# Attention by pairs of key blocks: two blocks' transposes back to back, their products with V together at the step's end

## The chip, the cores and the metric

The kernel runs on one core of a Trainium2 chip. The metric is the device time of one execution in microseconds (us), given as the median of several runs; less is better.

## The reference

One layer of a two-branch attention block on 1024 positions of width 1024, all in float32. An input projection feeds branch A (latent attention, 8 heads, mask by chunks of 64) and branch B (attention with a forget gate, 8 heads, causal). What the change touches is the inner part of both:

```
for i in range(seq // Q_BLOCK):            # blocks of 128 queries
    lo, hi = i * Q_BLOCK, (i + 1) * Q_BLOCK
    s = (scores of q[lo:hi] with k[:hi]) * scale   # + bias in branch B
    s = jnp.where(mask, s, -jnp.inf)
    p = jax.nn.softmax(s, axis=-1)
    outs.append(jnp.einsum('bhqk,bkhd->bqhd', p, v[:, :hi]))
```

The outputs are multiplied by SiLU gates, projected, merged with sigmoid gates, projected once more and added to the input.

## The kernel before, in words

Every large product is made of float32r matmuls: operands are split into a high and a low part, and three (sometimes two) products are summed in PSUM. The program first normalizes the input and makes the latents (0 to about 290 us of the profile), then runs the attention of all 16 heads with the remaining projections between (about 290 to 812 us), then the rest of the projections and the output.

**Order of the work.** All engines follow the order in which the program is written. `attention` (L1254) walks over 16 heads and, for each, over 12 *turns*, one for each block of keys `j`: four for the first half of the queries (`g` = 0, blocks 0 to 3) and eight for the second (`g` = 1, blocks 0 to 7). A counter of modelled TensorE time (`pe_time`) is advanced by each matmul; a turn is due every `STEP` = 2490 of it, and `fill_to` (L142) puts matmuls of the projections (tiles `f`) between until the time is reached. So TensorE always has projection work behind the attention work, in a fixed order.

**A turn** (`turn`, L1195) transposes the block of P (the softmax's result, rows of queries) with one transpose for each of up to four query blocks, into a bank of PSUM `pt` (tag `t`, two buffers). ScalarE copies it to the high part of `pp` (L1207), VectorE makes the low part (L1208). `product` multiplies both with V into the bank `o`, one or two turns later, from a queue in `attention`. For the blocks on the diagonal (the last four of each half) only 4, 3, 2 and 1 query blocks remain, so tiles are 512, 384, 256 and 128 columns wide.

**The scores of later rows** are made between the turns by `scores` (L1158), in an order that the table `ahead` gives: rows of 128 queries, 0 to 3 of a head in the PSUM tile `n` (one buffer), 4 to 7 in the tile `s` (1024 columns, **one buffer** during attention). After the matmuls VectorE takes the maximum (L1181), ScalarE the exponential from PSUM into SBUF with the sum (L1187, two records on the engine: ACTIVATE and ACTIVATION_READ_ACCUMULATOR), VectorE the reciprocal (L1190), GpSimd scales (L1191). The exponential is issued by the first `next` on the generator that `scores` returns, the scaling by the second. In the loop before, the first `next` comes in the turn after the scores, right after that turn's transposes and copy, and new scores are begun after it:

```
pr = self.turn(n, g, j)
last, finish = finish, None
if last:
    next(last)            # exponential of the scores begun a turn ago
...
if k in ahead and n + ahead[k][0] < N:
    finish = self.scores(n + ahead[k][0], ahead[k][1])
```

The rows 4, 5, 6 of the next head and 7 of this one, which share the one `s` buffer, are begun in turns 7, 9, 11 and 1: two turns apart.

**Preparation of the next heads' q and k** (`prep_a`, `prep_b`; groups of four transposes into a `t` bank, tiles `qt`, `kt`) is called at turns given by the table `parts`.

Of the kernel before, what the change touches and what calls it, by code (L numbers as in the profile page):

```python
# [74 lines left out]
class Net:  # L75
# [966 lines left out]

    def prep_a(self, n):

        nc, U = self.nc, self.U
# [144 lines left out]
            yield  # L1192
        return finish()

    def turn(self, n, g, j):  # L1195
# [2 lines left out]
        i0 = max(j - 4 * g, 0)
        c0 = i0 * P
        pt = self.bank("t", f"pt{n}_{g}{j}")  # L1200
        for i in range(i0, 4):
            self.transpose(pt[:, i * P:(i + 1) * P], self.p[n, 4 * g + i][:, j * P:(j + 1) * P])
        if j >= 4 * g:
            (self.U if g else self.Hs).put(self.p.pop((n, j)))
        pp = self.U.get([P, 2, 512], F32R, f"pp{n}_{g}{j}")
        ph, pl = pp[:, 0], pp[:, 1]
        nc.scalar.copy(ph[:, c0:], pt[:, c0:])  # L1207
        nc.vector.tensor_tensor(out=pl[:, c0:], in0=pt[:, c0:], in1=ph[:, c0:].bitcast(F32), op=ALU.subtract)  # L1208

        def product():  # L1210
            v = self.v[n]
            if j == 0:
                self.o = self.bank("o", f"o{n}_{g}")
            o = self.o
            self.U.put(pp)
            if j < 4 * g + 3:
                self.mm(o[:, c0:], v[:, j], ph[:, c0:], j == 0, False)
                self.mm(o[0:64, c0:], v[:, j, 0:64], pl[:, c0:], False, False)
                return
            self.mm(o[0:64, c0:], v[:, j, 0:64], pl[:, c0:], False, False)  # L1220
            self.mm(o[:, c0:], v[:, j], ph[:, c0:], False, True)
# [32 lines left out]
    def attention(self):  # L1254
        nc, N = self.nc, len(self.seq)
        preps = {n: self.prep_a(n) if n < 8 else self.prep_b(n) for n in range(0, N, 2)}
        parts = {}
# [4 lines left out]
        next(preps[0])
        self.fill_to(self.pe_time + 10000)
        self.load_v(0)
        for i in range(5):
# [4 lines left out]
            if i == 4:  # L1270
                self.gate_sum((4, 5))
                self.gate_load((6, 7))
        for c, i in enumerate((0, 4, 1, 5, 2, 3, 6)):
# [16 lines left out]
            self.fill_to(self.pe_time + 1500)  # L1290
        due = self.pe_time
        ahead = {1: (0, 7), 2: (1, 0), 4: (1, 1), 6: (1, 2), 8: (1, 3), 7: (1, 4), 9: (1, 5), 11: (1, 6)}
        for n in range(N):
            for k in range(12):
                g, j = (0, k) if k < 4 else (1, k - 4)
                due += self.STEP
                pr = self.turn(n, g, j)
                last, finish = finish, None
                if last:
                    next(last)  # L1300
                if (n, k) in parts:
                    next(preps[parts[n, k]])
                if k in ahead and n + ahead[k][0] < N:
                    finish = self.scores(n + ahead[k][0], ahead[k][1])
                if last:
                    next(last)
                if k == 2 and 0 < n < N - 1:
# [1 line left out]
                for at, call, a in self.extra:
                    if at == (n, k):  # L1310
                        call(*a)
                self.fill_to(due - 600)
                if k not in (1, 5):
                    while queue:
                        queue.pop(0)()
                self.fill_to(due)
                queue.append(pr)
# [38 lines left out]
    def build(self):  # L1356
# [35 lines left out]
        self.extra += [((3, 0), self.gate_row, ())]  # L1392
# [125 lines left out]
```

## Time and profile before

| | |
|---|---|
| Runs | 966.36, 964.3, 965.95 us; median 965.95 |
| Profiled execution | 961.75 us; span from first to last instruction 959.9 us |
| TensorE matmul (PE) | 947.9 us busy, 99% of the span, granted clock 0.999 |
| VectorE (DVE), ScalarE (ACT), GpSimd (POOL) | 66%, 50%, 22% of the span |
| Chain that ended last | PE 92%, DMA 3%, DVE 2%, ACT 2% |

How to read it: matmuls are pipelined, so a record of one lasts longer (0.40 us for 512 columns) than the distance from one start to the next (0.23 us); prices of TensorE are therefore read from starts. The name of a group is out<-in without buffer numbers. "Idle before" is time in which the engine did nothing before an instruction, with what ended it.

### The profile page before, as it was taken

How to read it: one execution, taken by the hardware profiler on the slowest of the kernel's cores; microseconds unless marked ns; L12 is line 12 of the kernel's file. 1: busy time of each engine (PE TensorE's matmuls, PEld its weight loads, DVE VectorE, ACT ScalarE, POOL GpSimd, SP SyncE). 2: the span in 40 equal slices, each digit the busy share in tenths (PEclk: the TensorE clock that was granted, in tenths of full speed). 3: DMA queues.
4: the chain of work that ended last, by engine and by line, in shares of the span. 5: the costliest groups of instructions: out<-in, count | busy, mean ns of one | idle time of the engine just before them, and what ended most of it. 6: DMA issues, size and time to landing. Idle time of an engine off the chain costs nothing.

```text
span 959.9 us, 14942 instructions
## 1 busy us (share of the span) xinstructions
PE 947.9 (99%) x5390; PEld 820.6 (85%) x5390; DVE 633.2 (66%) x1379; ACT 477.3 (50%) x959; POOL 208.1 (22%) x260
## 2 busy tenths in 40 slices
PE   7999999999999999999999999999999999999998
PEld 7999999998878888888888888888888888888887
DVE  3977877778366667657667676667676766495222
ACT  7776624543245556556555566465565654143000
POOL 0022142200012222221233333232333220046000
PEclk9999999999999999999999999999999999999999
DMA  9831132951973225235332232222421554644321
GB/s 340 334 98 45 51 114 62 323 216 40 343 232 110 88 67 132 71 95 133 99 91 68 66 101 89 80 88 89 120 70 46 186 186 154 238 147 138 103 88 66
DMA packets 79961, 124.96 MB, mean 130 GB/s; under 512 B 5928, under 2 KB 47536, under 8 KB 79888
## 3 DMA queue, kind: packets, MB, share of 16 engines
q1 hardware_dynamic: 79888, 124.01, 39.4%
q8 instruction: 42, 0.69, 0.3%
q14 instruction: 31, 0.25, 0.1%
HBM read 88.33 MB, written 35.66 MB: 129 GB/s over the span
## 4 chain that ended last, share of the span: by engine, by line
PE 92%; DMA 3%; DVE 2%; ACT 2%; issue 1%; SPq 1%; POOL 0%; ACTq 0%; DVEq 0%; POOLq 0%
PE f L127 36%; PE out L127 9%; PE s L127 9%; PE b L127 8%; PE o L127 7%; PE pt L136 6%; PE q L127 3%; PE ckv L127 2%; PE kv L127 2%; PE cq_s L127 2%; PE bv L127 1%; PE cq_t L127 1%; DMA x_u<-in_x 1%; PE pada L127 1%; DMA va_d<-vhl_u 1%
## 5 line engine op out<-in xcount | busy, mean ns | idle before, releaser
L1207 ACT CAST pp_u<-pt 128x512 fp32r<-128x512 f32 x192 | 91.9, 479 | 171.1 <-PE pt L136 155.0
L1208 DVE TENSOR_TENSOR pp_u<-pt,pp_u 128x512 fp32r<-128x512 f32 x192 | 106.7, 556 | 84.8 <-ACT pp_u L1207 81.9
L127 PE MATMUL f<-hT_lo,hi_f_u 128*128 128x512 f32 x384 | 153.6, 400 | 0.0
L127 PE MATMUL f<-hT_hi,lo_f_u 128*128 128x512 f32 x384 | 153.4, 399 | 0.0
L127 PE MATMUL f<-hT_hi,hi_f_u 128*128 128x512 f32 x384 | 153.1, 399 | 0.0
L127 PE MATMUL s<-k_u,q_u 96*128 96x512 f32 (+6 forms) x480 | 116.8, 362 | 0.9 <-DMA k_u<-kr_d 0.9
L1181 DVE TENSOR_REDUCE nm<-s 128x1 f32<-128x128 f32 (+7 forms) x128 | 97.0, 758 | 4.4
L1191 POOL TENSOR_SCALAR p_u<-p_u,rs 128x640 f32<-128x640 f32 (+1 forms) x64 | 64.3, 1004 | 164.1 <-DVE rs L1190 119.0
L1191 POOL TENSOR_SCALAR p_h<-p_h,rs 128x128 f32<-128x128 f32 (+1 forms) x64 | 41.7, 652 | 247.3 <-DVE rs L1190 208.2
L127 PE MATMUL o<-pp_u,v_u 128*128 128x512 f32 (+7 forms) x384 | 94.2, 340 | 0.0
L127 PEld LDWEIGHTS s<-k_u,q_u 96*128 96x128 f32 (+2 forms) x480 | 77.0, 190 | 7.3 <-issue 0.9
L127 PEld LDWEIGHTS f<-hT_hi,hi_f_u 128*128 128x128 f32 x384 | 72.4, 189 | 12.1
L127 PEld LDWEIGHTS f<-hT_hi,lo_f_u 128*128 128x128 f32 x384 | 72.4, 189 | 11.2
L127 PEld LDWEIGHTS f<-hT_lo,hi_f_u 128*128 128x128 f32 x384 | 72.5, 189 | 11.1
L127 PEld LDWEIGHTS o<-pp_u,v_u 128*128 128x128 f32 (+1 forms) x384 | 61.8, 161 | 19.5
L127 PE MATMUL b<-hi_b_u,hT_hi 128*128 128x256 f32 x256 | 73.1, 285 | 0.0
L127 PE MATMUL b<-hi_b_u,hT_lo 128*128 128x256 f32 x256 | 72.4, 283 | 0.0
L127 PE MATMUL b<-lo_b_u,hT_hi 128*128 128x256 f32 x256 | 72.4, 283 | 0.0
L136 PEld LDWEIGHTS pt<-ident,p_u 128*128 128x128 f32 x416 | 52.7, 140 | 16.7
L136 PE MATMUL pt<-ident,p_u 128*128 128x128 f32 x416 | 66.2, 272 | 0.0
L1187 ACT ACTIVATE p_u<-s,nm 128x640 f32<-128x640 f32 (+1 forms) x64 | 61.5, 961 | 4.3 <-DVE nm L1181 3.2
L127 PE MATMUL out<-lo_wo_u,hT_hi 128*128 128x512 f32 (+1 forms) x136 | 51.2, 377 | 0.0
(318 smaller groups left out, 2073.1 us busy)
## 6 DMA issues: line engine op xcount, KB each, us to landing
raw_f_u<-in_w_t SPq DMA_DIRECT2D x24, 512.0 KB
wada_u<-in_w_ada SPq DMA_DIRECT2D x16, 512.0 KB
mg_d<-th_h SPq DMA_DIRECT2D x32, 256.0 KB
mg_h<-mg_d SPq DMA_DIRECT2D x32, 256.0 KB
x_u<-in_x SPq DMA_DIRECT2D x8, 512.0 KB
raw_b_u<-in_w_b SPq DMA_DIRECT2D x8, 512.0 KB
raw_wg_u<-in_w_gate SPq DMA_DIRECT2D x8, 512.0 KB
va_d<-vhl_u SPq DMA_DIRECT2D x8, 512.0 KB
```

The source lines that it names most:

```text
L127: self.nc.tensor.matmul(out, lhsT=l, rhs=r, start=start, stop=stop)
L136: self.nc.tensor.transpose(out=out, in_=in_, identity=self.ident)
L1181: nc.vector.tensor_reduce(out=nm, in_=sv, axis=AX.X, op=ALU.max, negate=True)
L1187: nc.scalar.activation(p[:, 0:w], sv, AF.Exp, bias=nm, accum_out=sm)
L1191: nc.gpsimd.tensor_scalar(out=p[:, 0:w], in0=p[:, 0:w], scalar1=rs, scalar2=0.0, op0=ALU.mult, op1=ALU.add)
L1207: nc.scalar.copy(ph[:, c0:], pt[:, c0:])
L1208: nc.vector.tensor_tensor(out=pl[:, c0:], in0=pt[:, c0:], in1=ph[:, c0:].bitcast(F32), op=ALU.subtract)
```

## The change

A head now has six *steps* instead of twelve turns; a step takes two blocks of keys. Steps 0 and 1 are blocks (0,1) and (2,3) of the first half; steps 2 to 5 are blocks (0,1), (2,3), (4,5), (6,7) of the second. At the start of a step the transposes of both blocks stand back to back, then the two copies and the two subtractions. For the last pair of a half the two narrow blocks (256 and 128 columns) are put side by side into one bank, so that one copy and one subtraction of 384 columns serve both. The products of both blocks are made at the end of the same step (800 of modelled time before it is due), right before the next step's transposes. The order of high and low product is low, high except for block 0. What follows a half (`ends`) is issued at the start of the next step, after the transposes.

The scores that are begun at a step's start get their exponential inside the step (at 2900 before it is due). In steps 3 and 4 a second row is begun at that point (`ahead2`: rows 4 and 5 of the next head, tile `s`); its exponential is issued at the start of the next step, after the transposes and copies. Row 6 (also tile `s`) is begun at the start of step 5. The table `parts` is written anew for the steps; the call of `gate_row` moves by one place.

```diff
+    def turn(self, n, g, js):
         nc, pa = self.nc, self.sp
+        shared = js[0] == 4 * g + 2
+        items, places = [], []
+        for j in js:
+            i0 = max(j - 4 * g, 0)
+            if not (shared and j == js[1]):
+                pt = self.bank("t", f"pt{n}_{g}{j}")
+                pp = self.U.get([P, 2, 512], F32R, f"pp{n}_{g}{j}")
+            for i in range(i0, 4):
+                at = P if shared and j == js[1] else i * P
+                self.transpose(pt[:, at:at + P], self.p[n, 4 * g + i][:, j * P:(j + 1) * P])
...
+        for pt, pp, c0 in places:
+            ph, pl = pp[:, 0], pp[:, 1]
+            nc.scalar.copy(ph[:, c0:], pt[:, c0:])
+            nc.vector.tensor_tensor(out=pl[:, c0:], in0=pt[:, c0:], in1=ph[:, c0:].bitcast(F32), op=ALU.subtract)
...
+                hi = lambda: self.mm(o[:, c0:], v[:, j], ph, j == 0, j == 4 * g + 3)
+                lo = lambda: self.mm(o[0:64, c0:], v[:, j, 0:64], pl, False, False)
+                for f in (hi, lo) if j == 0 else (lo, hi):
+                    f()
...
-        ahead = {1: (0, 7), 2: (1, 0), 4: (1, 1), 6: (1, 2), 8: (1, 3), 7: (1, 4), 9: (1, 5), 11: (1, 6)}
+        blocks = [(0, (0, 1)), (0, (2, 3)), (1, (0, 1)), (1, (2, 3)), (1, (4, 5)), (1, (6, 7))]
+        ahead = {0: (0, 7), 1: (1, 0), 2: (1, 1), 3: (1, 2), 4: (1, 3), 5: (1, 6)}
+        ahead2 = {3: (1, 4), 4: (1, 5)}
...
         for n in range(N):
+            for d, (g, js) in enumerate(blocks):
+                due += 2 * self.STEP
+                product = self.turn(n, g, js)
+                if finish:
+                    next(finish)
+                if ends:
+                    ends()
+                if (n, d, 0) in parts:
+                    next(preps[parts[n, d, 0]])
+                first = begin(n, ahead.get(d))
+                if finish:
+                    next(finish)
...
+                self.fill_to(due - 2900)
+                if first:
+                    next(first)
+                if (n, d, 1) in parts:
+                    next(preps[parts[n, d, 1]])
+                finish = begin(n, ahead2.get(d))
+                rest(n, 2 * d + 1)
+                self.fill_to(due - 1500)
+                if first:
+                    next(first)
+                self.fill_to(due - 800)
+                ends = product()
```

**TensorE from block 5's scores to the scores of row 6, head 5.** `pt_16`, `pt_17` are the transposes of blocks 6 and 7 in the second half, `s_6` the scores of row 6 of head 6, `f` projections, `o` products with V. Before:

```order
L136 MATMUL pt_16_5559<-ident,p_6_u_311_5256 128x128
L136 MATMUL pt_16_5559<-ident,p_7_u_315_5313 128x128
L127 MATMUL f_00_5498<-hT_lo,hi_f_u_319_5381 128x512
...
L127 MATMUL o_1_5463<-pp_15_u_328_5535,v_u_286_4966 128x384
L127 MATMUL o_1_5463<-pp_15_u_328_5535,v_u_286_4966 64x384
L127 MATMUL f_00_5498<-hT_hi,hi_f_u_319_5381 128x512
L136 MATMUL pt_17_5581<-ident,p_7_u_315_5313 128x128
L127 MATMUL s_6_5586<-k_6_u_306_5211,q_6_u_288_4987 128x512
```

Now (the last `o` and the start of step 5):

```order
L127 MATMUL o_1_5395<-pp_15_u_316_5463,v_u_282_4953 64x384
L127 MATMUL o_1_5395<-pp_15_u_316_5463,v_u_282_4953 128x384
L136 MATMUL pt_16_5517<-ident,p_6_u_301_5204 128x128
L136 MATMUL pt_16_5517<-ident,p_7_u_304_5256 128x128 x2
L127 MATMUL s_6_5526<-k_6_u_297_5177,q_6_u_278_4928 128x512
```

The eleven matmuls between the transposes of block 6 and those of block 7 are gone, and `s_6` stands directly behind the transposes.

**TensorE in step 4 of the same head,** blocks 4 and 5, with the scores of rows 3 (tile `n`) and 5 (tile `s`). Before, 13 rows lie between `pt_14` and `s_5`, and a turn's start between `s_3` and `s_5`. Now:

```order
L136 MATMUL pt_15_5462<-ident,p_7_u_304_5256 128x128
L127 MATMUL s_3_5473<-k_6_u_297_5177,q_6_u_278_4928 128x512
L127 MATMUL s_3_5473<-k_6_u_298_5178,q_6_u_278_4928 128x512
L127 MATMUL s_3_5473<-k_6_u_297_5177,q_6_u_279_4929 128x512
L127 MATMUL f_00_5486<-hT_hi,hi_f_u_310_5368 128x512
L127 MATMUL f_00_5486<-hT_lo,hi_f_u_310_5368 128x512
L127 MATMUL f_00_5486<-hT_hi,lo_f_u_311_5369 128x512
L127 MATMUL s_5_5494<-k_6_u_297_5177,q_6_u_278_4928 128x384 x2
```

From the first transpose of the step to `s_5` stand seven transposes, three matmuls of row 3 and three of `f`.

**ScalarE over the same two steps.** The ACTIVATE rows with `p_` are the exponentials of the scores, the CAST rows the copies of `pt`. Before:

```order
L1207 CAST pp_14_u_327_5508<-pt_14_5503 128x512
L1187 ACTIVATE p_4_u_325_5488,sm_4_5511<-s_4_5478,nm_4_5486 128x640
L1207 CAST pp_15_u_328_5535<-pt_15_5531 128x384
L1187 ACTIVATE p_3_h_123_5520,sm_3_5538<-s_3_5513,nm_3_5518 128x512
L1207 CAST pp_16_u_330_5562<-pt_16_5559 128x256
L1187 ACTIVATE p_5_u_329_5550,sm_5_5565<-s_5_5540,nm_5_5548 128x768
L1207 CAST pp_17_u_331_5583<-pt_17_5581 128x128
```

Now:

```order
L1217 CAST pp_14_u_315_5457<-pt_14_5456 128x512
L1217 CAST pp_15_u_316_5463<-pt_15_5462 128x384
L1188 ACTIVATE p_4_u_314_5439,sm_4_5471<-s_4_5429,nm_4_5437 128x640
L1188 ACTIVATE p_3_h_123_5480,sm_3_5490<-s_3_5473,nm_3_5478 128x512
L1217 CAST pp_16_u_320_5518<-pt_16_5517 128x384
L1188 ACTIVATE p_5_u_319_5504,sm_5_5524<-s_5_5494,nm_5_5502 128x768
L1188 ACTIVATE p_6_u_321_5536,sm_6_5544<-s_6_5526,nm_6_5534 128x896
```

The exponential of row 4 stands behind two copies instead of one, that of row 5 behind the copy of the pair (6,7).

## Rows read from the trace of the kernel before

**Rows 1.** Busy time by stretch: busy us (instructions) of each engine, granted clock.

```profile
0.00:40.00 40.00, 34.32 (x232) 32.94 (x232) 23.93 (x62) 30.57 (x53) 0.34 (x6) 1.00 0.96 365
40.00:292.00 252.00, 249.89 (x1716) 234.88 (x1715) 184.62 (x479) 122.65 (x225) 43.07 (x68) 1.00 0.47 156
292.00:552.00 260.00, 259.69 (x1412) 217.40 (x1411) 172.28 (x372) 150.79 (x322) 67.39 (x80) 1.00 0.31 89
552.00:812.00 260.00, 259.75 (x1378) 215.15 (x1377) 182.70 (x372) 150.18 (x320) 72.31 (x90) 1.00 0.34 107
812.00:960.00 148.00, 144.19 (x659) 120.19 (x657) 69.65 (x98) 23.09 (x41) 25.03 (x16) 0.99 0.39 135
```

**Rows 2.** Timeline of TensorE: start us, us, instruction; narrow products, then one group of transposes.

```profile
402.65 0.39 PE L127 MATMUL f<-hT_lo,hi_f_u 128*128 128x512 f32 x1
402.88 0.33 PE L127 MATMUL o<-pp_u,v_u 128*64 128x128 f32 x2
403.05 0.45 PE L127 MATMUL f<-hT_hi,lo_f_u 128*128 128x512 f32 x1
403.34 0.40 PE L127 MATMUL f<-hT_hi,hi_f_u 128*128 128x512 f32 x1
403.57 0.60 PE L136 MATMUL pt<-ident,p_u 128*128 128x128 f32 x4
403.93 0.48 PE L127 MATMUL f<-hT_lo,hi_f_u 128*128 128x512 f32 x1
404.25 0.40 PE L127 MATMUL f<-hT_hi,lo_f_u 128*128 128x512 f32 x1
```

**Rows 3.** Groups of weight loads, by form, 292 to 812 us.

```profile
L136 PEld LDWEIGHTS pt<-ident,p_u 128*128 128x128 f32 x416 | 52.7, 140 | 16.7
L127 PEld LDWEIGHTS s<-k_u,q_u 96*128 96x128 f32 x258 | 41.5, 189 | 3.1 <-ACT p_u L1187 0.2
L127 PEld LDWEIGHTS o<-pp_u,v_u 128*128 128x128 f32 x192 | 36.0, 188 | 11.3
```

**Rows 4.** Timeline of all engines: three transposes; a copy that waited for its transposes.

```profile
425.05 0.49 PE L136 MATMUL pt<-ident,p_h 128*128 128x128 f32 x3
...
433.31 0.60 PE L136 MATMUL pt<-ident,p_u 128*128 128x128 f32 x4
...
433.94 0.59 ACT L1207 CAST pp_u<-pt 128x512 fp32r<-128x512 f32 x1 [0.16 <-PE pt L136]
```

**Rows 5.** Timeline of ScalarE over one head's last turns.

```profile
442.41 0.58 ACT L1207 CAST pp_u<-pt 128x512 fp32r<-128x512 f32 x1 [0.75 <-PE pt L136]
443.02 0.58 ACT L1187 ACTIVATE p_h<-s,nm 128x384 f32<-128x384 f32 x1
...
444.66 0.59 ACT L1207 CAST pp_u<-pt 128x512 fp32r<-128x512 f32 x1
445.14 0.80 ACT L1187 ACTIVATE p_u<-s,nm 128x640 f32<-128x640 f32 x1
445.83 0.20 ACT L1187 ACTIVATION_READ_ACCUMULATOR p_u<-s,nm 128x1 f32 x1
447.24 0.48 ACT L1207 CAST pp_u<-pt 128x384 fp32r<-128x384 f32 x1 [1.20 <-PE pt L136]
447.61 0.69 ACT L1187 ACTIVATE p_h<-s,nm 128x512 f32<-128x512 f32 x1
...
449.99 0.91 ACT L1187 ACTIVATE p_u<-s,nm 128x768 f32<-128x768 f32 x1
450.78 0.20 ACT L1187 ACTIVATION_READ_ACCUMULATOR p_u<-s,nm 128x1 f32 x1
```

**Rows 6.** Timeline of TensorE: the scores of row 6 in that head.

```profile
452.13 1.46 PE L127 MATMUL s<-k_u,q_u 96*128 96x512 f32 x6
```

**Rows 7.** Timeline: TensorE resumes after two waits ahead of the attention.

```profile
233.37 0.50 PE L127 MATMUL bv<-lo_b_u,hT_hi 128*128 128x512 f32 x1 [1.00 <-DVE lo_b_u L116]
...
233.72 0.40 PE L127 MATMUL bv<-hi_b_u,hT_lo 128*128 128x512 f32 x1
```

**Rows 8.** Timeline: from the end of a sum's read to the reciprocal.

```profile
425.24 0.21 ACT L1187 ACTIVATION_READ_ACCUMULATOR p_u<-s,nm 128x1 f32 x1
...
425.55 0.16 DVE L1190 RECIPROCAL rs<-sm 128x1 f32<-128x1 f32 x1
```

**Rows 9.** Timeline of ScalarE: projection work ahead of a copy.

```profile
422.34 0.60 ACT L989 ACTIVATE th_h<-f 128x512 f32<-128x512 f32 x1 [2.20 <-PE f L127]
...
422.83 1.13 ACT L115 CAST hi_f_u<-raw_f_u 128x512 fp32r<-128x512 f32 x2
```

**Rows 10.** Groups of VectorE by form, 292 to 812 us: the subtraction.

```profile
L1208 DVE TENSOR_TENSOR pp_u<-pt,pp_u 128x512 fp32r<-128x512 f32 x96 | 66.1, 689 | 37.4 <-ACT pp_u L1207 36.2
```

**Rows 11.** Timeline of VectorE: the maximum of a row 5.

```profile
448.49 0.96 DVE L1181 TENSOR_REDUCE nm<-s 128x1 f32<-128x768 f32 x1
```

More of the change, by code (lines that the diff above doesn't have):

```diff
@@ L1193, in scores @@
         return finish()
-    def turn(self, n, g, j):
+    def turn(self, n, g, js):
         nc, pa = self.nc, self.sp
[L1198 to L1208, printed above, removed]
+        shared = js[0] == 4 * g + 2
[8 more added lines that the diff above has]
+                self.transpose(pt[:, at:at + P], self.p[n, 4 * g + i][:, j * P:(j + 1) * P])
+            if j >= 4 * g:
+                (self.U if g else self.Hs).put(self.p.pop((n, j)))
+            items.append((j, i0 * P, pp, P if shared and j == js[1] else i0 * P))
+            if not (shared and j == js[0]):
+                places.append((pt, pp, P if shared else i0 * P))
+        for pt, pp, c0 in places:
+            ph, pl = pp[:, 0], pp[:, 1]
+            nc.scalar.copy(ph[:, c0:], pt[:, c0:])
+            nc.vector.tensor_tensor(out=pl[:, c0:], in0=pt[:, c0:], in1=ph[:, c0:].bitcast(F32), op=ALU.subtract)
@@ L1210, in product @@
         def product():
             v = self.v[n]
[L1212 to L1221, printed above, removed]
+            for j, c0, pp, p0 in items:
+                ph, pl = (pp[:, e, p0:p0 + 512 - c0] for e in range(2))
+                if j == 0:
+                    self.o = self.bank("o", f"o{n}_{g}")
+                o = self.o
+                hi = lambda: self.mm(o[:, c0:], v[:, j], ph, j == 0, j == 4 * g + 3)
+                lo = lambda: self.mm(o[0:64, c0:], v[:, j, 0:64], pl, False, False)
+                for f in (hi, lo) if j == 0 else (lo, hi):
+                    f()
@@ L1222, in product, with ends @@
+            for pp in dict((id(x[2]), x[2]) for x in items).values():
+                self.U.put(pp)
+            return ends if js[1] == 4 * g + 3 else None
+        def ends():
+            o, v = self.o, self.v[n]
             if g:
@@ L1258, in attention @@
         for n in range(2, N, 2):
-            for at in ((n - 2, 0), (n - 2, 3), (n - 2, 5), (n - 2, 6), (n - 2, 10), (n - 1, 3)):
-                parts[at] = n
-        finish, queue = None, []
+            for at in ((n - 3, 4, 1), (n - 2, 1, 0), (n - 2, 3, 1), (n - 2, 4, 0), (n - 2, 5, 0), (n - 1, 1, 0)):
+                parts[max(at, (0, 0, 0))] = n
+        finish = None
         next(preps[0])
@@ L1291, in attention @@
         due = self.pe_time
-        ahead = {1: (0, 7), 2: (1, 0), 4: (1, 1), 6: (1, 2), 8: (1, 3), 7: (1, 4), 9: (1, 5), 11: (1, 6)}
-        for n in range(N):
[L1294 to L1307, printed above, removed]
-                    self.load_v(n + 1)
[L1309 to L1317, printed above, removed]
@@ L1318, in attention, with begin, rest @@
-        queue.pop(0)()
+        blocks = [(0, (0, 1)), (0, (2, 3)), (1, (0, 1)), (1, (2, 3)), (1, (4, 5)), (1, (6, 7))]
+        ahead = {0: (0, 7), 1: (1, 0), 2: (1, 1), 3: (1, 2), 4: (1, 3), 5: (1, 6)}
+        ahead2 = {3: (1, 4), 4: (1, 5)}
+        ends = None
+        def begin(n, at):
+            return self.scores(n + at[0], at[1]) if at and n + at[0] < N else None
+        def rest(n, k):
+            for at, call, a in self.extra:
+                if at == (n, k):
+                    call(*a)
@@ new lines, in attention @@
+        for n in range(N):
+            for d, (g, js) in enumerate(blocks):
[10 more added lines that the diff above has]
+                    next(finish)
+                if d == 1 and 0 < n < N - 1:
+                    self.load_v(n + 1)
+                rest(n, 2 * d)
+                self.fill_to(due - 2900)
[10 more added lines that the diff above has]
+                ends = product()
@@ L1321, in output @@
+        ends()
     def output(self):
@@ L1391, in build @@
         self.extra += [((15, 10), self.load_y, (1, 2)), ((15, 11), self.split_y, (1, 2))]
[L1392 removed]
+        self.extra += [((3, 1), self.gate_row, ())]
         with tc.manual_schedule():
```

## Prediction

> **What bounds the kernel now.** I read the busy time by stretch first [rows 1]: over the attention (292 to 812 us) TensorE is busy 259.69 and 259.75 of 260 us at a granted clock of 1.00, while ScalarE and VectorE reach some 150 and 180. TensorE does not wait there, so nothing that only relieves another engine can shorten the kernel, and each stall that is added to TensorE lengthens it by its own size: after the attention 144.19 of 148 us are busy again, with no idle time that could take a delay up. The question is therefore what the change does to TensorE's own work, and whether it makes TensorE wait.
>
> The second view is the timeline of TensorE, for prices from start to start [rows 2]. A 512-column matmul takes 0.23 us (403.34 to 403.57). Four transposes and one `f` take 403.57 to 404.25, 0.68 us; less 0.23 that is 0.11 for each transpose, and nothing else: the matmul after them looks long (0.32) only because its record starts early, under the last transpose. Two 128-column products and an `f` take 402.88 to 403.34, 0.46 us, where their columns would need 0.23 + 2 x 0.058 = 0.345: 0.115 us is lost, because a narrow matmul does not cover the weight load of the next one.
>
> **TensorE's work, part by part.** The number of transposes (576), of products and of scores is unchanged. *Back to back:* transposes cost 0.11 us each in a group of four, with no remainder for the turn to matmuls and back, so 96 groups of eight cost what 192 of four did: 0, at most 0.01 x 96 = 1 us gained. *Narrow products:* the last product of the shared pair is now followed by a transpose instead of `f` in 31 of 32 places. A transpose's weight load is recorded with 140 ns, that of a product or of `f` with 188 to 189 [rows 3], so about 0.05 of the 0.115 us goes: 31 x 0.05 = -1.6 us (bounds 0 and 31 x 0.115 = -3.6). I take the -1.6, since the records differ by just that. *Copies and subtractions:* 32 fewer of each; ScalarE and VectorE are not the bound, so 0. *Order high/low:* the wide products cover the weight load either way, 0.
>
> **What now waits.** Rows 4, 5 and 6 of the scores share the one buffer `s`, so the first matmul of a row waits for the exponential of the row before. Such a wait hardly exists in the trace (0.2 us in all, the last figure of the second of rows 3), because two turns lay between: row 5's exponential ends its sum's read at 450.98 [rows 5], row 6 starts at 452.13 [rows 6]. In the changed program row 6 stands right behind the transposes of step 5, and row 5's exponential right behind the copy that waits for these transposes. TensorE runs its matmuls in order, so everything behind row 6 stands too.
>
> *Step 5,* from the start T of its first transpose. Three transposes are done at T + 0.49 and the copy starts 0.03 later (433.31 + 0.60 to 433.94) [rows 4]. From the start of a 384-column copy to that of the exponential behind it: 0.37 (447.24 to 447.61). From the 768-column exponential's start to the read of its sum: 0.79; that read: 0.20 [rows 5]. The hop to the waiting engine: 0.10, as from the end of such a read (425.45) to the reciprocal (425.55) [rows 8]; no row shows it for TensorE, so between 0.03 and 0.20. A matmul that resumes has its weight load exposed: 0.35 to the next start instead of 0.23, so 0.12 more [rows 7]. Sum: T + 0.49 + 0.03 + 0.37 + 0.79 + 0.20 + 0.10 + 0.12 = T + 2.10. Without the wait row 6 would follow three transposes, at T + 0.33. The stall is 1.77 us. In seven heads (0, 2, ... 12) four transposes `kt` stand between, and it is 1.77 - 0.44 = 1.33. Over the 15 heads that have a successor: 8 x 1.77 + 7 x 1.33 = 23.5 us.
>
> *Step 4* (row 5 waits for row 4's exponential, now behind two copies). Four transposes end at T + 0.60, the first copy starts at T + 0.63; 0.48 to 0.61 to the next start (444.66 to 445.14, 442.41 to 443.02), I take 0.55; second copy 0.37; the 640-column exponential 0.69 to its sum's read, 0.20 for that [rows 4, 5]; 0.10 and 0.12 as above: T + 2.66. TensorE comes there after seven transposes, row 3 and three `f` (two passes and four `f` in branch B): 0.77 + 0.69 + 0.69 = T + 2.15, in three heads with one `f` less T + 1.92. Stall: 12 x 0.51 + 3 x 0.74 = 8.3 us. Bounds: 0, if ScalarE is 0.5 us quicker here, and 15 x 1.2, if projection work stands ahead of the copy.
>
> The other buffers hold. Row 4 (step 3) and row 7 (step 0) come a step or more after the exponential that they wait for. The two `t` banks: `qt` and `kt` at a step's start fall into steps 1 and 5, where the pair uses one bank; `qt` in step 3 stands behind eight transposes, row 2 and four `f`, 0.87 + 0.52 + 0.92 = 2.3 us, and its bank is free after the first subtraction, at 0.63 + 0.59 + 0.69 = 1.9 us [rows 4, 10]. Row 5's maximum (0.96 us [rows 11]) has the time of five `f` or more and four products, some 1.9 us, before step 5 begins. The load of `ks` (512 KB) on SP's queue is issued one step (5.4 us) ahead, not four turns; it takes 1.4 us at the 365 GB/s and 5.9 us at the 89 GB/s of rows 1, and if it is 0.5 us late, `kt` stands ahead of row 6 and that falls into a wait that is there anyway: 0. Before, all this had its cover in TensorE's own work between two turns; that cover is what the grouping takes away.
>
> *Sum:* 23.5 + 8.3 - 1.6 = +30.2 us. The profiled execution takes 961.75 us (span 959.9), 4.2 below the median of the runs; on that median the forecast is 965.95 + 30.2 = **996 us** (992 for a profiled execution).
>
> **A rule against the change.** The waits above would leave TensorE idle some 2.1 us in every 33. In 40 to 292 us, which holds waits of up to 1.00 us on TensorE [rows 7], the granted clock stayed at 1.00, that is at 2.4 GHz [rows 1], and I let it stay there. The Trainium skill, TensorE: Matmul & The Clock Gate, section "A second HAM failure mode: psum-queue depth-cycling", says that short idle times between groups of matmuls, from cycling through PSUM banks, can make the clock fall to half again and again. By the trace the sum is +30 us; by that rule it would be far more, and it is a rival below.
>
> **The rivals.**
> - *Only step 5 waits.* ScalarE's overlap of copy and exponential varies by 0.13 us in rows 5, and with some more of it row 4's exponential is done when TensorE comes. Then 23.5 - 1.6: 988 us.
> - *ScalarE comes late.* In some heads a tanh and a weight split stand ahead of the copies; they take 0.60 + 1.13 us [rows 9]. If that delays seven of the 15 heads by the whole of it, +12: 1008 us.
> - *The turn costs more than it shows (faster).* A turn from transposes to products could hide a loss that the pipelined records do not show: at most a transpose's record and the late start after it, 0.27 + 0.09 = 0.36 us. 96 turns less would save 34.6 us, more than the stalls cost: 996 - 34.6 = 961.6 us. It decides from 30.2 / 96 = 0.31 us a turn. Against it: 0.68 us for four transposes and an `f` leave 0.01.
> - *The stalls are not there,* since the exponential somehow ends in time: 965.95 - 1.6 = 964.3 us. Against it stands the order on both engines.
> - *The clock falls.* If the two steps with waits ran at half clock in 15 heads, 15 x 2 x 5.4 us (520 us of attention over 96 steps) would be added: about 1158 us.
>
> **How the numbers follow.** Both waits as worked out 0.55; only step 5: 0.20; late ScalarE 0.16; half clock 0.02; costly turns 0.05; no stalls 0.02. A change under 0.2% (1.9 us) cannot be told from none. Slower: 0.55 + 0.20 + 0.16 + 0.02 = 0.93; faster 0.05 (the costly turns); within 0.2%: 0.02 (no stalls). The forecast's own range is 985 to 1006: the hop and the copies' overlap, 0.1 to 0.2 us at 30 places, and 0 to -3.6 for the narrow products. With the first two rivals the range is 978 to 1012.
>
> **What the profile after would show.** TensorE waiting for `p_u` (ScalarE's exponential) some 30 times, in two sizes: 1.2 to 1.8 us ahead of the scores of 512 + 384 columns, and 0.3 to 0.8 ahead of those of 384 + 384; some 30 us more of attention and an unchanged time before 292 us and after it; transposes still 0.11 us apart in groups of eight; the copies 32 fewer. The forecast is wrong if TensorE is as busy in the attention as before, if its waits end on VectorE or a transfer, or if transposes become cheaper in larger groups.

## The result, and the profile after

| | before | after |
|---|---|---|
| Median of 4 runs each | 965.12 us (962.91 to 966.36) | **1010.18 us** (1007.32 to 1010.9) |
| Ratio after / before | | 1.0464, 95% interval 1.0434 to 1.0494 |
| Profiled execution | 961.75 us | 1007.32 us, span 1005.5 us |
| Mean granted clock of the profiled span | 0.999 | 0.998 (0.995 in each of the other three runs) |

The change costs 45 us; 30 were forecast (996 us, range 978 to 1012). The busy time by stretch after, in the columns of [rows 1]:

```profile
40.00:292.00 252.00, 248.85 (x1712) 234.04 (x1711) 184.53 (x479) 122.29 (x224) 42.55 (x67) 1.00 0.46 153
292.00:574.00 282.00, 263.99 (x1401) 218.53 (x1400) 167.35 (x355) 146.86 (x305) 65.36 (x80) 0.99 0.29 84
574.00:858.00 284.00, 267.66 (x1398) 220.46 (x1397) 180.99 (x361) 149.22 (x307) 71.60 (x91) 1.00 0.31 99
858.00:1005.00 147.00, 143.79 (x657) 119.85 (x656) 68.74 (x96) 22.65 (x40) 25.00 (x16) 1.00 0.38 133
```

The stretches ahead of the attention and behind it are as long and as busy as before. The attention went from 520 to 566 us, and TensorE, which was busy in all of it, is now idle for 34 us of it. Its waits (engine, what waited, for what, line: us, times, longest us), and the chain that ended last by engine (before, PE had 92% of it):

```profile
PE s L127 <- ACT p_u L1188: 25.3, 25, 2.1
PE pt L136 <- DVE q_u L1129: 3.4, 3, 1.2
PE pt L136 <- DVE q_u L1075: 2.9, 3, 1.1
PE pt L136 <- DVE s L1180: 1.1, 1, 1.1
```

```profile
PE 81%; ACT 9%; DVE 6%; issue 2%; DMA 1%; SPq 0%; POOL 0%; ACTq 0%; DVEq 0%
```

The first line is the wait that was forecast, for ScalarE's exponential. The next three were not: transposes of P that wait, in seven heads, for a bank of `t` that the low part of q gives back (in the last line the profile names the instruction behind that low part). These idle times are smaller than the losses, since the exposed weight load after each is not idle time. So the losses below are summed from starts: what lies between two starts of TensorE beyond 0.231 us for 512 columns and 0.109 us for a transpose.

**Step 5, as forecast.** Timeline of TensorE, then of ScalarE, in the step 5 of head 5 (start us, us, instruction, idle time before it and what ended it):

```profile
500.11 0.49 PE L136 MATMUL pt<-ident,p_u 128*128 128x128 f32 x3
502.12 1.49 PE L127 MATMUL s<-k_u,q_u 96*128 96x512 f32 x6 [1.52 <-ACT p_u L1188]
503.45 0.40 PE L127 MATMUL f<-hT_hi,lo_f_u 128*128 128x512 f32 x1
...
500.69 0.48 ACT L1217 CAST pp_u<-pt 128x384 fp32r<-128x384 f32 x1 [2.04 <-PE pt L136]
501.07 0.91 ACT L1188 ACTIVATE p_u<-s,nm 128x768 f32<-128x768 f32 x1
501.86 0.20 ACT L1188 ACTIVATION_READ_ACCUMULATOR p_u<-s,nm 128x1 f32 x1
```

From T = 500.11: copy at T + 0.58, exponential 0.38 later, its sum's read 0.79 later, row 6 at T + 2.01 (0.06 after the read's end), and 0.12 for the exposed weight load: T + 2.13, where the forecast had T + 2.10.

**Step 4, partly not.** Timelines of TensorE, VectorE and ScalarE at the end of step 3 and in step 4 of head 4:

```profile
459.35 0.60 PE L136 MATMUL pt<-ident,p_u 128*128 128x128 f32 x4
460.83 0.52 PE L136 MATMUL pt<-ident,p_u 128*128 128x128 f32 x3 [0.88 <-DVE q_u L1075]
...
462.76 1.31 PE L127 MATMUL s<-k_u,q_u 96*128 96x384 f32 x6 [0.25 <-ACT p_u L1188]
...
455.71 0.68 DVE L1218 TENSOR_TENSOR pp_u<-pt,pp_u 128x512 fp32r<-128x512 f32 x1
...
456.54 0.56 DVE L1182 TENSOR_REDUCE nm<-s 128x1 f32<-128x384 f32 x1
459.17 1.52 DVE L1075 SCALAR_TENSOR_TENSOR q_u<-qt,vqa,q_u 64x512 fp32r<-64x512 f32 x2 [2.06 <-ACT q_u L1073]
...
457.20 0.58 ACT L1188 ACTIVATE p_h<-s,nm 128x384 f32<-128x384 f32 x1 [1.63 <-DVE nm L1182]
...
457.77 1.36 ACT L1073 ACTIVATE q_u<-qt,vqa 64x512 fp32r<-64x512 f32 x2
```

Row 5's scores wait for row 4's exponential (0.25 us), as forecast. Ahead of that the transposes of block 5 wait 0.88 us for a bank of `t`. It holds `qt`, q's second group, called in the middle of step 3. VectorE takes its low part at 459.17 to 460.69, and had been idle 2.06 us until then: ScalarE makes the high part first, and its two instructions stand behind row 2's exponential, which waits for row 2's maximum, which stands behind the second subtraction. A chain over two in-order queues, not a busy engine, holds the bank.

**Step 0, not forecast.** VectorE, ScalarE and TensorE from step 5 of head 4 to step 0 of head 5, then ScalarE and TensorE in step 0 of head 0:

```profile
469.29 1.51 DVE L1075 SCALAR_TENSOR_TENSOR k_u<-kt,vec,k_u 64x512 fp32r<-64x512 f32 x2 [1.60 <-ACT k_u L1073]
...
471.02 1.09 DVE L1182 TENSOR_REDUCE nm<-s 128x1 f32<-128x896 f32 x1
...
467.89 1.37 ACT L1073 ACTIVATE k_u<-kt,vec 64x512 fp32r<-64x512 f32 x2
472.21 1.01 ACT L1188 ACTIVATE p_u<-s,nm 128x896 f32<-128x896 f32 x1 [2.96 <-DVE rs L1191]
...
468.05 1.49 PE L127 MATMUL s<-k_u,q_u 96*128 96x512 f32 x6 [1.03 <-ACT p_u L1188]
...
473.36 1.65 PE L127 MATMUL s<-k_u,q_u 96*128 96x512 f32 x6
```

```profile
296.51 1.03 ACT L1188 ACTIVATE p_u<-s,nm 128x896 f32<-128x896 f32 x1
...
297.68 1.65 PE L127 MATMUL s<-k_u,q_u 96*128 96x512 f32 x6 [2.07 <-ACT p_u L1188]
```

Row 6's scores are done at 469.54, but on VectorE `kt`'s low part stands ahead of their maximum until 470.80; it waits for ScalarE's high part, which stands behind row 5's exponential. So row 6's exponential starts only as the next head begins, and row 7 is late by 0.3 to 0.7 us in each odd head (0.4 here). It is the group in step 5 that does this, not TensorE's wait there: the odd heads, without `kt`, wait longer in step 5 (1.8 us), and row 7 of the head behind them does not wait. Head 0 differs: its row 6 is made before the loop, so the exponential is issued in step 0 behind both copies, and row 7 waits for it, 2.4 us by starts. Another 0.5 us there is a transpose that waits for GpSimd.

**The clock, once.** Stretches of the attention around the step 5 of head 3 (length; busy us of PE, PEld, DVE, ACT, POOL; granted clock):

```profile
424.50:430.50 6.00, 4.85 (x24) 3.61 (x22) 3.59 (x9) 3.03 (x8) 1.49 (x2) 1.00 0.01 3
430.50:432.30 1.80, 1.31 (x6) 1.17 (x7) 0.13 (x1) 0.44 (x2) 0.00 (x0) 1.00 0.00 0
432.30:436.20 3.90, 3.90 (x12) 3.05 (x11) 1.44 (x4) 1.10 (x2) 1.66 (x2) 0.56 0.00 0
```

After the wait of 1.8 us there, matmuls stand 0.43 us apart instead of 0.23 from 432.81 to 436.20, 3.4 of the 3.9 us of the last line, at 1.2 GHz: 1.6 us lost. This was one of eight equal waits. The other three runs have a mean clock of 0.995 instead of 0.998; 0.003 of 1008 us are 3 us, about what separates them from the profiled run.

| TensorE's losses, us over 16 heads | forecast | trace |
|---|---|---|
| Step 5: row 6 waits for row 5's exponential | 23.5 | 23.5 |
| Step 4: row 5 waits for row 4's exponential | 8.3 | 8.2 |
| Step 4: block 5's transposes wait for the bank of `qt` (7 heads) | 0 | 8.8 |
| Step 0: row 7 waits for row 6's exponential (2.4 in head 0); a transpose of head 0 for GpSimd (0.5) | 0 | 6.4 |
| Step 2: row 1 waits for row 0's exponential (heads 9, 11, 12); products in head 14 | 0 | 1.1 |
| One stretch at half clock | 0 | 1.6 |
| Narrow products | -1.6 | -0.7 |

That is 48.9, against 45.6 between the two profiled executions; before, 0.5 of step 0 and 0.6 of the first two rows stood there already, so the table finds some 2 us more than were measured, and these stay unexplained.

### The profile page after: what moved, and what is told of

Read it like the earlier page. It is cut to its first block, busy times and chain, and to the rows that moved or that the text cites. A ratio compares the mean times of both kernels' runs of the same rounds, so it can differ in the third digit from the quotient of the medians.

```text
span 1005.5 us, 14856 instructions
## 1 busy us (share of the span) xinstructions
PE 958.5 (95%) x5390; PEld 825.5 (82%) x5390; DVE 625.0 (62%) x1347; ACT 470.9 (47%) x927; POOL 204.8 (20%) x260
## 4 chain that ended last, share of the span: by engine, by line
PE 81%; ACT 9%; DVE 6%; issue 2%; DMA 1%; SPq 0%; POOL 0%; ACTq 0%; DVEq 0%
PE f L127 30%; PE out L127 9%; PE b L127 8%; PE s L127 7%; PE o L127 6%; PE pt L136 4%; PE bv L127 4%; ACT p_u L1188 3%; PE q L127 3%; PE ckv L127 2%; PE kv L127 2%; PE cq_s L127 2%; ACT pp_u L1217 1%; DVE nm L1182 1%; DVE pp_u L1218 1%
## 5 line engine op out<-in xcount | busy, mean ns | idle before, releaser
L127 PE MATMUL f<-hT_hi,lo_f_u 128*128 128x512 f32 x384 | 151.3, 394 | 0.0
L127 PE MATMUL f<-hT_lo,hi_f_u 128*128 128x512 f32 x384 | 150.8, 393 | 0.0
L1218 DVE TENSOR_TENSOR pp_u<-pt,pp_u 128x512 fp32r<-128x512 f32 (+1 forms) x160 | 95.8, 632 | 87.3 <-ACT pp_u L1217 86.9
L127 PE MATMUL s<-k_u,q_u 96*128 96x512 f32 (+6 forms) x480 | 116.9, 362 | 28.7 <-ACT p_u L1188 25.3
L1217 ACT CAST pp_u<-pt 128x512 fp32r<-128x512 f32 (+1 forms) x160 | 81.4, 546 | 90.8 <-PE pt L136 88.5
L1192 POOL TENSOR_SCALAR p_h<-p_h,rs 128x128 f32<-128x128 f32 (+1 forms) x64 | 37.3, 583 | 263.5 <-DVE rs L1191 206.3
L127 PE MATMUL o<-pp_u,v_u 128*128 128x512 f32 (+7 forms) x384 | 84.6, 342 | 0.0
L1188 ACT ACTIVATE p_h<-s,nm 128x128 f32<-128x128 f32 (+1 forms) x64 | 33.8, 528 | 92.4 <-DVE nm L1182 62.5
L127 PEld LDWEIGHTS o<-pp_u,v_u 128*128 128x128 f32 (+1 forms) x384 | 59.1, 161 | 21.8 <-issue 0.4
L136 PE MATMUL pt<-ident,p_u 128*128 128x128 f32 x416 | 57.5, 274 | 7.3 <-DVE q_u L1129 3.4
L136 PEld LDWEIGHTS pt<-ident,p_u 128*128 128x128 f32 x416 | 48.0, 140 | 13.7 <-issue 5.5
```

What stands on the lines that cost most here:

```text
L127: self.nc.tensor.matmul(out, lhsT=l, rhs=r, start=start, stop=stop)
L136: self.nc.tensor.transpose(out=out, in_=in_, identity=self.ident)
L1188: nc.scalar.activation(p[:, 0:w], sv, AF.Exp, bias=nm, accum_out=sm)
L1192: nc.gpsimd.tensor_scalar(out=p[:, 0:w], in0=p[:, 0:w], scalar1=rs, scalar2=0.0, op0=ALU.mult, op1=ALU.add)
```

## Experiments

All times are medians, the intervals 95% intervals of the ratio to the kernel before in runs beside them (medians 962.96 to 964.30 us).

| | us | ratio to before |
|---|---|---|
| the change (above) | 1010.18 | 1.0464 |
| e1_exp_first | 995.64 | 1.0327 (1.0297 to 1.0357) |
| e2_rows67_mid | 1010.5 | 1.0513 (1.0463 to 1.0562) |
| e3_q_group | 1025.82 | 1.0642 (1.0614 to 1.0671) |
| e4_all | 1017.09 | 1.0554 (1.0527 to 1.0581) |
| e5_before_row6 | 986.7 | 1.0241 (1.0225 to 1.0257) |
| e6_split | 987.7 | 1.0254 (1.0228 to 1.028) |
| e7_first_row6 | 1001.99 | 1.0401 (1.0384 to 1.0418) |
| e8_q_odd | 988.32 | 1.0256 (1.0234 to 1.0278) |
| e9_row7_late | 977.73 | 1.0138 (1.012 to 1.0156) |
| e10_q_alone | 1000.91 | 1.0393 (1.0376 to 1.0411) |
| e11_row7_alone | 1011.08 | 1.0499 (1.0475 to 1.0524) |
| e12_row7_order | 965.35 | 1.0031 (1.0014 to 1.0047) |

### The first four: undoing waits one by one

e1_exp_first:

```diff
-                product = self.turn(n, g, js)
                 if finish:
                     next(finish)
+                product = self.turn(n, g, js)
```

> The changed kernel (45 us above the kernel before), with one move: the exponential of rows 4 and 5 is issued ahead of the next step's transposes and copies, not behind them. Theory A (the one buffer of rows 4 to 6, together with ScalarE's order, makes the waits): the 23.5 us in step 5 and the 8.2 us in step 4 go, since row 5's maximum (0.96 us) and exponential (0.99 us) fit into the 2.5 us that remain of the step; 45 - 31.7 = 13 us above the kernel before, about 978 us, and TensorE's waits for p_u fall below 5 us. Theory B (the grouping itself costs: eight transposes in a row, two copies at once): within 5 us of the changed kernel, 1005 to 1010 us.

Between the two theories: some 14 us came back instead of 32. By starts, step 5 fell from 23.5 to 14.8 us and row 5's wait in step 4 from 8.2 to 3.6. The odd heads of step 5 behave as theory A says (1.8 to 0.34 in most). In the even heads 0.8 to 1.1 stay, since the wait for `qt` makes row 5 late, so its maximum and exponential too; in heads 6 and 12 a 2.1 us wait is followed by half clock.

e2_rows67_mid:

```diff
-        ahead = {0: (0, 7), 1: (1, 0), 2: (1, 1), 3: (1, 2), 4: (1, 3), 5: (1, 6)}
-        ahead2 = {3: (1, 4), 4: (1, 5)}
+        ahead = {1: (1, 0), 2: (1, 1), 3: (1, 2), 4: (1, 3)}
+        ahead2 = {0: (0, 7), 3: (1, 4), 4: (1, 5), 5: (1, 6)}
```

> The changed kernel, with rows 6 and 7 begun in the middle of steps 5 and 0 (as rows 4 and 5 are in steps 3 and 4), ScalarE's order as it is. Theory A: row 6 comes to its buffer 2.3 us into step 5, after row 5's exponential (2.0 us): the 23.5 us go, and the 3.5 us of row 7 in the odd heads; row 7 then meets row 6's exponential behind two copies, as in step 4, for 0 to 0.5 us in 16 heads: 45 - 27 + 5 = 23 us above the kernel before, about 988 us. Theory B: within 5 us of the changed kernel.

The 23.5 us of step 5 went (0.2 left), and as much appeared in step 2. TensorE's largest wait is now:

```profile
PE pt L136 <- POOL p_u L1192: 24.3, 14, 2.6
```

Row 7 is scaled too late for the transposes of step 2. In head 5 its exponential is done at 480.79, but its reciprocal stands on VectorE behind `kt`'s low part and row 0's maximum until 484.02, and GpSimd scales from 484.37 to 485.49. The theory was right on the wait that it named and blind to the next reader.

e3_q_group, `(n - 2, 3, 1)` made `(n - 2, 1, 1)` in the table `parts`:

> The changed kernel, with the second group of q (tile qt) called in the second half of step 1 instead of step 3, so that the pair of blocks 4 and 5 in step 4 does not find a bank of t still held by it. Theory C (in even heads pt_15 waits for the two subtractions q_u that VectorE makes late from qt): the 8.8 us of step 4 go, 1001 us, and nothing comes in step 2. Rivals: VectorE is as late in step 1, and the wait only moves to step 2 (1010 us); or the wait comes from eight transposes that need two banks at once whatever stands there (1010 us).

The first rival: the wait in step 4 is gone and stands in step 2, twice as long, and the kernel is 15 us slower still.

```profile
PE pt L136 <- DVE q_u L1129: 10.0, 4, 2.7
PE pt L136 <- DVE q_u L1075: 7.1, 3, 2.7
```

e4_all: the moves of e1 and e3, and row 7 in `ahead2[0]`.

> The changed kernel, with three moves together: the exponential of rows 4 and 5 (and 7) ahead of the transposes, the second group of q in step 1, row 7 begun in the middle of step 0. Grouped transposes, the shared bank and the products at the step's end stay. Theories A and C: 31.7 + 8.8 + 3.5 us of the 45 go, and head 0's 2.9 us perhaps: 965 to 966 us, the kernel before within 3 us. Theory B: well above, 990 us or more. The forecast's rival of a turn that costs more than it shows: below 955 us, as the stalls would have covered a gain.

Wrong by 50 us: steps 0, 3 and 4 lose under 3 us together, but step 2 loses 41 (step 1 some 5, step 5 some 8). Both late readers of e2 and e3 meet there, and the clock falls behind them. Timeline of TensorE in step 2 of head 4, and stretches around it:

```profile
450.26 0.33 PE L136 MATMUL pt<-ident,p_u 128*128 128x128 f32 x1 [1.09 <-POOL p_u L1192]
452.31 1.05 PE L136 MATMUL pt<-ident,p_u 128*128 128x128 f32 x4 [1.72 <-DVE q_u L1075]
```

```profile
449.00:452.30 3.30, 0.49 (x3) 0.16 (x2) 1.60 (x3) 2.19 (x5) 1.12 (x1) 1.00 0.20 75
452.30:456.20 3.90, 3.89 (x14) 3.43 (x15) 2.83 (x7) 1.98 (x4) 0.37 (x1) 0.56 0.04 11
```

Half clock followed in all seven heads with `qt` in step 1.

### Is it the grouping? Two controls

e5_before_row6, the kernel before with one entry moved:

```diff
-        ahead = {1: (0, 7), 2: (1, 0), 4: (1, 1), 6: (1, 2), 8: (1, 3), 7: (1, 4), 9: (1, 5), 11: (1, 6)}
+        ahead = {1: (0, 7), 2: (1, 0), 4: (1, 1), 6: (1, 2), 8: (1, 3), 7: (1, 4), 9: (1, 5), 10: (1, 6)}
```

> The kernel before, in turns, nothing grouped, with one entry of the table moved: row 6 is begun one turn after row 5 instead of two. TensorE then meets row 5's exponential in flight, behind the two transposes of block 6 (0.22 us) and without the eleven matmuls that stood between. Theory A (the distance of the rows that share the buffer makes the wait, whether transposes are grouped or not): 1.7 us in the 8 heads without kt, 1.25 in the 7 with it, 22 us, about 987 us. Theory B (the grouping costs by itself): within 2 us of the kernel before.

Theory A: 23.7 us between the medians where 22 were expected, 986.7 us where 987 was written. TensorE's waits hold one new line, and the timelines of TensorE and ScalarE at turn 10 of head 5 show a wait of row 6 that [rows 6] do not have:

```profile
PE s L127 <- ACT p_u L1187: 18.7, 15, 2.1
```

```profile
489.43 1.49 PE L127 MATMUL s<-k_u,q_u 96*128 96x512 f32 x6 [1.41 <-ACT p_u L1187]
...
488.38 0.91 ACT L1187 ACTIVATE p_u<-s,nm 128x768 f32<-128x768 f32 x1
489.17 0.20 ACT L1187 ACTIVATION_READ_ACCUMULATOR p_u<-s,nm 128x1 f32 x1
```

So the stall of step 5 needs no grouping: two rows that share the one buffer, one turn apart, are enough.

e6_split, the kernel e8_q_odd below with a projection matmul between the two blocks' transposes:

```diff
         for j in js:
...
+            if js[1] == j:
+                self.fill_to(self.pe_time + 1)
             for i in range(i0, 4):
```

> As e8_q_odd, with one projection matmul put between the transposes of a step's two blocks (96 places; the number of matmuls stays). Against e8_q_odd of the same call: if the turn from transposes to matmuls and back costs 0.36 us that pipelined records hide (the rival of the forecast), 96 x 0.36 = 35 us more; if transposes cost 0.11 us in groups of four and of eight alike, within 2 us of it.

987.7 against 988.32 us, where 35 us more would be plain. By starts, from the last transpose of the first block to the first of the second, with the `f` between, 0.346 us pass (median of 96), and 0.109 + 0.231 make 0.340: 96 more turns cost some 0.6 us. The rival of a turn that costs 0.36 us is out, and with it any such gain from fewer turns.

### Following the waits to the end

e7_first_row6 is e1 with row 6 in `ahead2[5]`.

> As e1_exp_first (33 us above the kernel before, 14.8 us of waits left in step 5), with row 6 begun in the middle of step 5; row 7 stays at the start of step 0. Theory A: the 14.8 us go and row 7 waits for row 6's exponential by 0 to 0.5 us more a head: 18 to 24 us above the kernel before, 981 to 987 us. Rival D (each wait that is taken away here comes back at the next thing that is late, as GpSimd's scaling of rows 6 and 7 ahead of step 2 did in e2_rows67_mid): 30 us or more above the kernel before.

Rival D: slower than e1 by 6 us. Step 5's losses fell from 14.8 to 1.4 us, and step 0's, row 7's wait above all, rose from 6.7 to 24.8.

e8_q_odd is e7 with q's two groups in the steps whose pair takes one bank:

```diff
-            for at in ((n - 3, 4, 1), (n - 2, 1, 0), (n - 2, 3, 1), (n - 2, 4, 0), (n - 2, 5, 0), (n - 1, 1, 0)):
-                parts[max(at, (0, 0, 0))] = n
+            q = ((0, 0, 0), (0, 1, 0), (0, 3, 1)) if n == 2 else ((n - 3, 3, 1), (n - 3, 5, 0), (n - 2, 1, 0))
+            for at in (*q, (n - 2, 4, 0), (n - 2, 5, 0), (n - 1, 1, 0)):
+                parts[at] = n
```

> As e7_first_row6, with the first group of q in step 5 of the head before and the second in step 1, the two steps whose pair takes one bank of t (head 0 keeps its places). In e3_q_group the second group stood in the middle of step 1 and its bank was still held in step 2; at a step's start the pair before it is one bank and the next pair comes a whole step later. Theory C: six of seven waits for q_u go, 7.5 us, and with them most of the waits of step 4 in the even heads (some 3 us): 10 us below e7_first_row6. Rival: VectorE or a load of q is late in the new place: no gain or a loss against it.

Theory C, with 13.7 us gained, of which by the mean clocks some 3 are less time at half clock: step 4's losses fell from 12.2 to 1.8, 1.6 of it in head 0, where nothing was moved. Nearly all that is left is one line, in 16 heads:

```profile
PE s L127 <- ACT p_u L1188: 19.7, 16, 2.2
```

e9_row7_late is e8 with row 7 behind projection matmuls (nine to eleven, 2.2 to 2.65 us in the trace, not the eight that were expected):

```diff
-                first = begin(n, ahead.get(d))
+                first = begin(n, ahead.get(d)) if d else None
...
-                self.fill_to(due - 2900)
+                self.fill_to(due - (2900 if d else 2400))
+                if d == 0:
+                    first = begin(n, (0, 7))
```

> As e8_q_odd (25 us above the kernel before, of which 25.5 are row 7's waits for row 6's exponential at the start of step 0, 0.97 to 2.4 us in 16 heads), with eight projection matmuls (1.85 us) between the transposes and row 7, and row 7's exponential right behind its scores in the same step. Theory A: the waits go to 1 to 3 us in all (heads 0, 13 and 15), and GpSimd's scaling of row 7, which was done 3.6 us before step 2, is still in time: 962 to 967 us, the kernel before within 0.3%. So nothing of the 45 us is the grouping's own. Rival D: GpSimd's scaling comes too late for step 2 as in e2_rows67_mid and e4_all: 20 us above. Rival B: what stays when the waits are gone is the price of the grouping, more than 5 us above.

Neither in size: row 7's waits went (25.5 to 0.6 us), GpSimd was in time, but 14.5 us appeared in step 2 by a third way. Timelines of VectorE and ScalarE in steps 0 and 1 of head 4, then of TensorE in step 2:

```profile
435.80 1.23 DVE L1182 TENSOR_REDUCE nm<-s 128x1 f32<-128x1024 f32 x1
438.44 0.16 DVE L1191 RECIPROCAL rs<-sm 128x1 f32<-128x1 f32 x1 [1.42 <-ACT p_u L1188]
438.75 0.56 DVE L1218 TENSOR_TENSOR pp_u<-pt,pp_u 128x384 fp32r<-128x384 f32 x1
440.02 1.51 DVE L1075 SCALAR_TENSOR_TENSOR q_u<-qt,vqa,q_u 64x512 fp32r<-64x512 f32 x2 [0.72 <-PE o L127]
...
437.14 1.12 ACT L1188 ACTIVATE p_u<-s,nm 128x1024 f32<-128x1024 f32 x1 [3.30 <-DVE nm L1182]
...
438.24 0.47 ACT L1217 CAST pp_u<-pt 128x384 fp32r<-128x384 f32 x1
438.60 1.38 ACT L1073 ACTIVATE q_u<-qt,vqa 64x512 fp32r<-64x512 f32 x2
...
441.68 0.63 PE L136 MATMUL pt<-ident,p_u 128*128 128x128 f32 x4 [1.24 <-DVE q_u L1075]
```

ScalarE stands 3.30 us before row 7's exponential, which waits for its maximum, and has the pair's copy and q's high part behind it, though their transposes were done by 435.8. The low part of q starts when the high part ends (439.98) and is late, and with it the bank. VectorE stands 1.42 us at row 7's reciprocal meanwhile, but that ends at 438.60, before the copy does (438.71), and costs nothing here; the profile puts the 0.72 us down to TensorE's `o`, which ends at the same time, but the low part reads the high part.

e10_q_alone and e11_row7_alone put one of these moves into the changed kernel by itself (e8's table; e9's place of row 7).

> The changed kernel with the places of the two groups of q of e8_q_odd and nothing else. Theory C: 7.5 of the 8.8 us ahead of pt_15 go; q's four transposes now fall into the wait of step 5 in seven odd heads (7 x 0.44 = 3 us less wait there); ScalarE's q_u make the exponential of row 6 later in those steps, 0.4 us more in seven heads of step 0: 8 us below the changed kernel, 1000 to 1004 us. Rival: as in e3_q_group the wait only moves: no gain.

As theory C says: 1000.91 us. Block 5's wait for `qt` fell from 8.8 to 1.4 us and step 5's from 23.5 to 21.0; step 0's rose from 6.4 to 10.5. With q's group now in step 5 of the odd heads, row 7 waits in the even heads 2 to 12 behind them too (0.3 to 0.7 us), although TensorE's own wait in those steps fell from 1.8 to 1.3 or 1.4 us: it is the group ahead of row 6's maximum that makes row 7 late.

> The changed kernel with row 7 begun 1.85 us later in step 0 and nothing else. Theory A: the 6.4 us that it waited there (2.9 in head 0, 0.3 to 0.7 in the odd heads) go to under 1.5 us: 5 us below the changed kernel, some 1005 us, 40 us above the kernel before. Rival D: they come back in step 2 as waits for GpSimd's scaling: no gain.

Rival D's outcome: no gain. Step 0's 6.4 us went to 0.8, and step 2 rose from 1.0 to 9.1. But no wait for GpSimd is new: what TensorE waits for there are VectorE's low parts of q and k, and row 0's exponential, as in e9.

e12_row7_order is e8 with row 7 behind seven to nine projection matmuls (`due - 2800` in step 0) and its exponential and reciprocal in step 1, after the q or k group:

```diff
+                if d == 1:
+                    next(row7)
+                    next(row7)
-                first = begin(n, ahead.get(d))
+                first = begin(n, ahead.get(d)) if d else None
...
-                self.fill_to(due - 2900)
+                self.fill_to(due - (2900 if d else 2800))
+                if d == 0:
+                    row7 = begin(n, (0, 7))
```

> As e9_row7_late (14 us above the kernel before; 14.5 us of it wait in step 2 for VectorE's q_u and k_u, which stand behind row 7's reciprocal, and that blocks VectorE 1.4 us for the exponential), with row 7's exponential and reciprocal issued in step 1, behind the copy, the subtraction and the q or k group, and row 7 begun 0.4 us earlier. Theory E (what is left is order on VectorE and ScalarE, none of it the grouping's): 10 to 12 us of the 14.5 go, some 2 us come back in step 0: 965 to 969 us. Rival D: GpSimd's scaling of row 7, now some 1.5 us later, misses step 2: no gain, 975 us or more.

Theory E: 965.35 against 964.30 us of the kernel before beside it, ratio 1.0031. In head 4 the copy (428.28) and q's high part (428.72) now stand ahead of row 7's exponential (430.13). The exponential and the reciprocal were moved together; that it is the exponential's place that counts is read from e9's trace alone. The attention lies within 292 to 812 us again (same columns as [rows 1]), and TensorE's largest wait in it is head 0's `qt`:

```profile
292.00:552.00 260.00, 258.41 (x1409) 218.51 (x1410) 170.29 (x355) 148.60 (x308) 67.69 (x82) 1.00 0.29 88
552.00:812.00 260.00, 259.38 (x1372) 216.57 (x1372) 178.16 (x355) 146.57 (x303) 69.65 (x88) 1.00 0.33 107
```

```profile
PE pt L136 <- DVE q_u L1075: 1.1, 1, 1.1
```

With pairs grouped, the shared bank and 32 copies fewer, but each row and group put where its reader is not kept waiting, the kernel is 0.3% slower than before. No version tried beats the kernel before.

## Why the prediction was right, and where it was short

**The number.** 45 us came where 30 were forecast. 1010 us lie above the forecast's own range (985 to 1006) and inside the stated one (978 to 1012) only because that was widened for the rival of a late ScalarE, which is not what happened; that much was luck. The two waits that were priced came in full, and some 15 us came from waits put at nothing.

**The bound was right.** TensorE had no idle time before [rows 1], nothing in the change made its work less, and the time grew by its stalls. The rival that a turn from transposes to matmuls costs more than it shows is refuted by e6_split, as the 0.68 us for four transposes and an `f` [rows 2] had said; transposes in groups of eight still start 0.109 us apart.

**Step 5 was right term by term:** 1.79 to 1.80 us in the seven odd heads, 1.30 to 1.36 in the seven even ones with `kt`, 1.74 in head 14, against 1.77 and 1.33 [rows 4, 5, 7, 8]. The hop, taken from the reciprocal of [rows 8] because no row had it for TensorE, was 0.06 and not 0.10 in the step shown, and the copy started 0.06 later than written; the two cancel. e5_before_row6 shows the cause apart from everything else.

**Step 4 was right in its sum, less in its parts:** 8.2 against 8.3 us, but 0.3 to 0.7 us in 14 heads, and 2.1 in head 14, where the second copy waits 1.34 us for VectorE.

**The narrow products** were mis-sized: 0.087 instead of 0.109 us are lost at each of 31 places, so -0.7 us and not -1.6; the difference of the recorded weight loads [rows 3] overstated it.

**The step that failed is "The other buffers hold".** It missed some 15 us, nearly all in two places. One of the forecast's own signs of being wrong, waits that end on VectorE, was there: 7.4 us of them beside 25.3 on ScalarE.

- On `t` it asked when `qt` finds its bank free, and was right that it does. It did not ask when `qt` gives the bank back. That happens behind row 2's maximum and exponential and four more instructions on two queues, as the timelines of step 4 show, and cost 8.8 us; e10_q_alone took 7.4 of them away by moving the groups of q alone.
- On `s` it said that row 7 comes a step or more after the exponential that it waits for. In head 0 it does not even by the order: there row 6's exponential is issued in step 0 itself, behind both copies (2.4 us). In the other heads it does, but that exponential runs only when row 6's maximum is there, and in the steps with `kt` this stands on VectorE behind `kt`'s low part, which waits for ScalarE. The forecast placed `kt` among TensorE's work and banks and did not ask what its two parts hold up on the other queues; e10_q_alone, with a group in step 5 of heads 0 to 12, has the wait in the head behind each of them.

**The clock** was a rival with 0.02 and 1158 us. It did fall, so the rival's mechanism exists; its price was 1.6 us in the profiled run and, by the mean clock, some 4 to 5 us in the others, because it fell behind few of the waits. The Trainium skill, TensorE: Matmul & The Clock Gate, section "A second HAM failure mode: psum-queue depth-cycling", has idle times between groups make the clock change back and forth; this trace agrees with that in kind, and e4_all most of all.

**Late ScalarE,** the rival of 1008 us, came out near the measured time by another way: tanh and weight split do stand ahead of the copies in the step shown (a `th` and a `hi_f` between 459.16 and 460.83), but its 12 us are not what was missing: in e10_q_alone, where the wait for the bank is gone, row 5 still loses only 0.4 to 0.7 us in 14 heads.

## What to carry to other kernels

When steps are grouped, list for every shared buffer both sides: who waits to get it, and which instruction gives it back, with everything that stands ahead of that one on its own queue. After each move, go through the list again for the next step: the waits that e2, e3, e7 and e11 removed came back, in full or more, at the next late reader; e1 and e10 kept some 14 and 7 to 9 us; and only four moves together (e12) brought the time back. Before looking for a cause in the regrouped work itself, put the suspected distance into the old kernel: one table entry gave 24 us there.

## What the runs showed of the hardware

The length of one wait does not tell whether half clock follows. One of eight equal 1.8 us waits of the changed kernel was followed by it, both 2.1 us waits of e1_exp_first were, and all seven places of e4_all with two waits in a row (in the one shown TensorE was busy 0.49 of 3.30 us). A wait of 2.6 us in step 2 of head 2 of e2_rows67_mid was not; busy time and granted clock in it and behind it:

```profile
374.70:377.30 2.60, 0.06 (x1) 0.00 (x0) 1.71 (x6) 0.94 (x3) 1.09 (x1) 1.00 0.83 314
377.30:381.30 4.00, 3.92 (x21) 3.41 (x22) 2.71 (x6) 2.05 (x5) 0.37 (x2) 1.00 0.02 8
```

In both stretches shown the granted clock was 0.56 over 3.9 us, and the one in the changed kernel cost 1.6 us beside the wait. And an engine whose instructions run in the order of issue is held by one that waits: in e9_row7_late ScalarE stood 3.30 us before one exponential, with a copy and q's high part behind it whose transposes were done, and TensorE waited 1.24 us for what came of them.
